# Sums of squares of q, k and the third layer's heads in two single passes

## The chip, the cores and the metric

The kernel runs on one core of a Trainium2 chip. A core has a matrix engine, TensorE (PE in the profile; its weight loads are PEld), and VectorE (DVE), ScalarE (ACT), GpSimd (POOL) and SyncE (SP), which issues the transfers. Each engine takes its instructions in its own order and waits on semaphores for the others. The metric is the time of one execution in device microseconds; less is better. Before the change it is 2625.27 us, the median of three runs (2624.19 to 2625.74).

## The reference

A stack of four layers on 1040 tokens (16 meta tokens and 1024 of the sequence) of width 1024, float32. Layers 0 and 3 are attention with a window of 128, layer 1 is an mLSTM, layer 2 an HGRN2 (a linear recurrence with gates). Each normalizes its input and adds its output to the stream h. What the change touches are normalizations of heads:

```python
def rmsnorm(x, g):
    xf = x.astype(jnp.float32)
    y = xf * lax.rsqrt(jnp.mean(xf * xf, axis=-1, keepdims=True) + EPS)
    return (y * g.astype(jnp.float32)).astype(x.dtype)
...
    # attention: 16 q heads and 4 k heads of 64
    q = rope(rmsnorm(q.reshape(bsz, lp, A_HEADS, A_HD), q_gain), pos)
    k = rope(rmsnorm(k.reshape(bsz, lp, A_KV, A_HD), k_gain), pos)
...
    # third layer: 8 heads of 128
    o = rmsnorm(o, o_gain.reshape(C_HEADS, C_DV)).reshape(bsz, lp, C_W)
```

## The kernel before

The stream is held transposed: 128 channels of a tile lie on the partitions, tokens along the free axis. Tokens are worked in three chunks of 400, 384 and 256 columns (for q in the last layer 384, 384, 256). A projection (`proj`) makes one tile of 128 output channels chunk by chunk; each chunk is 24 products of TensorE in four steps.

A product of float32 operands is taken at full precision. To go faster, most products are made from rounded parts: `split` has ACT round a tile to the type float32r (`h`) and DVE subtract that from the tile and round the rest (`l`), and three single passes (h by h, h by l, l by h) take the place of one full-precision product. Weights (`wh`, `wl`), the normalized input (`uh`, `ul`) and the operands of the output projections (`yh`, `yl`, three buffers each, `YS`) are made so. Split operands of the output projections are made by `ysplit` in `proj_out`.

A sum of squares over the channels of a head is a product of the squares with a matrix of ones, since the channels lie on the partitions. Before the change there are these:

- line 364, the norm of a layer's input, with `ones`, at full precision;
- line 516 (`stat_q`), q tiles: the squares of a block of 128 tokens are the stationary operand and two columns of the mask of heads the moving one, so the result has tokens on the partitions and two columns, one for each head of the tile; full precision;
- line 525 (`stat`), k tiles: the mask of heads (block diagonal, 128 by 128) by the squares of a chunk; full precision;
- line 983, the heads of the second layer: `ones` in float32r by two rounded parts of the squares, two single passes;
- line 1259 (`o_stat`), the heads of the third layer: `ones` by the squares, full precision.

TensorE's order is written out by hand: a list of steps with costs, into which other steps are put a given time after a chunk's end (`D_K` for k tiles, `D_Q` for q tiles, in the planner's ns, counted in the costs of the steps that stand between). For a k tile, the chunk's last product is followed by `evac` (ACT: line 492 scales, line 493 squares; four transfers turn halves for the rotation), after 2000 by `stat` (line 525, then Ln and Exp on ACT, lines 338 and 339), after 4000 by `rope` (DVE, lines 530 to 534, with a table `cs` that has one buffer), after 6000 by the turn (`k_split`: four casts and two copies on ACT, lines 444, 445 and 447, and two subtractions on DVE, line 446). For a q tile it is 2000 for the table, 3000 for `stat_q`, 4000 for `rope`, 6000 for the turn (`q_split`, lines 463 and 464). The factor that `stat_q` makes is read only in the scores of the softmax (line 629). The order on ACT, DVE, POOL and SP is made by a scheduler from the order of the steps and their priorities.

The first k tile and the first two q tiles of an attention layer are made in its head, together with the norm of the layer's input, chunk by chunk. A norm unit (`Norm.unit`, lines 386, 194, 195) makes `uh` and `ul` of one of eight tiles of a chunk. The second k tile is made later, between the softmax steps, its three chunks one right behind the other. In the third layer `o_evac` copies a head's output and squares it (lines 1251 and 1253), and `o_stat` follows at the next place for it.

Of the kernel before, what the change touches and what calls it, by code (L numbers as in the profile page):

```python
# [9 lines left out]
F32 = mybir.dt.float32  # L10
# [5 lines left out]
P = 128  # L16
# [29 lines left out]
D_V, V_AHEAD, K_AHEAD = 1500.0, 3000.0, 12000.0  # L46
PARTS = 4
FIRST = (0.2, 0.8, 0.85), (0.2, 0.75, 0.8)
D_K = 2000.0, 4000.0, 6000.0
D_Q = 2000.0, 3000.0, 4000.0, 6000.0  # L50


MM = 1.0 / 2.4
# [58 lines left out]
def hybrid_kernel(ctx: ExitStack, tc: tile.TileContext, ins, out, layers=(0, 1, 2, 3)):  # L112
# [41 lines left out]
    s.preload_act_table_set("natural_log_exp_and_others")  # L154

    ident = cpool.tile([P, P], F32, name="ident")
    ones = cpool.tile([P, P], F32, name="ones")
    v.memset(ones, 1.0)
    ngain = cpool.tile([P, 4, KT], F32, name="ngain")
    eps = cpool.tile([P, 1], F32, name="eps")  # L160
    v.memset(eps, EPS)
# [24 lines left out]
    def meta_tokens(mix):  # L186

        um[0] = z = mix.tile([P, KT, 48], F32R, name=nm("um"))
        g.memset(z.bitcast(F32), 0.0)
        for o, src in ((0, uh), (32, ul)):  # L190
            g.tensor_copy(z[:, :, o : o + NMETA], src[:, :, :NMETA].bitcast(F32))

    def split(src, h, l):
        s.copy(h, src)  # L194
# [98 lines left out]
    def proj_out(src0, src1, y, chunks=CHUNKS, fin=None, inrow=False):  # L293
        st = {}

        def pre0():
            st[0] = weights(src0, "o", inrow=inrow)

        def pre1():
            st[1] = weights(src1, "o", inrow=inrow)  # L300

        groups = []
        for n, (c0, cn) in enumerate(chunks):
            grp = []

            def ysplit(k, n=n, c0=c0, cn=cn):
                def fn():
                    yh, yl = (tpool.tile([P, 400], F32R, tag=z, name=nm(z), bufs=YS)[:, :cn] for z in ("yh", "yl"))
                    split(y(k)[:, c0 : c0 + cn], yh, yl)
                    st["y", n, k] = yh, yl  # L310

                return [0.0, hi(fn), None]

            def product(m, k, n=n, c0=c0, cn=cn):
                h, l = st[m // 4]
                mc = slice((m % 4) * P, (m % 4 + 1) * P)
                if k == 0:
                    st["p", n, m] = psj()
                acc = st["p", n, m]
                yh, yl = st["y", n, k]  # L320
                for i, (a, b) in enumerate(((h, yh), (h, yl), (l, yh))):
                    pe.matmul(acc[:, :cn], a[:, k, mc], b,  # L322
                              start=(k == 0 and i == 0), stop=(k == 1 and i == 2))
                if k == 1:
                    v.tensor_tensor(x[:, m, c0 : c0 + cn], x[:, m, c0 : c0 + cn], acc[:, :cn], op=ALU.add)  # L325
# [90 lines left out]
    def layer_a(i, j, first, last, fin):  # L416
# [3 lines left out]

        def enter():
            R["mix"] = mix = new_mix()
            R["masks"] = masks = mix.tile([P, 384], F32, name=nm("masks"))
            sp.dma_start(masks, ins["a_masks"])
            R["cons"] = cons = mix.tile([P, 18], F32, name=nm("cons"))
            sp.dma_start(cons, ins["a_cols"][j])
            v.tensor_scalar(cons[:, 0:1], cons[:, 0:1], -0.125, None, op0=ALU.mult)
            v.tensor_scalar(cons[:, 2:18], cons[:, 2:18], -1.0, None, op0=ALU.mult)
# [57 lines left out]
        def qk_proj(src, gcol, work, fsplit, ch, t=None):  # L486
# [11 lines left out]
            def finish(n, c0, cn):  # L498
                def factors():
                    b0, bn = CHUNKS[n]  # L500
                    if R.get("cs", (None,))[0] != n:
                        R["cs"] = n, R["mix"].tile([P, 2, 400], F32, tag="cs", name=nm("cs"), bufs=1)
                        sp.dma_start(R["cs"][1][:, :, :bn], ins["rope"][:, :, b0 : b0 + bn].rearrange("a p t -> p a t"))
                    late[n] += (R["cs"][1][:, :, c0 - b0 : c0 - b0 + cn],)

                def stat_q():

                    sq = late[n][1]
                    nb = len(CHUNK_BLOCKS[n])
                    R["rq", t, n] = rq = R["mix"].tile([P, 2 * nb], F32, tag=f"rq{n}", name=nm("rq"), bufs=4)  # L510
                    st = psa()
                    for k, b in enumerate(CHUNK_BLOCKS[n]):
                        if last and b == 0:
                            continue
                        q0 = blk(b)[0] - c0
                        pe.matmul(st[:, 2 * k : 2 * k + 2], sq[:, q0 : q0 + P], R["masks"][:, 0:P:64], start=True, stop=True)  # L516
                    z = slice(2 if last and n == 0 else 0, 2 * nb)
                    s.activation(rq[:, z], st[:, z], AF.Ln, bias=eps, scale=1.0 / 64)
                    s.activation(rq[:, z], rq[:, z], AF.Exp, scale=-0.5)

                def stat():
                    factors()
                    sq = late[n][1]
                    st = psa()
                    pe.matmul(st[:, :cn], R["masks"][:, 0:P], sq, start=True, stop=True)
                    rstd_from(st, sq, cn, 64)

                def rope():
                    dst, sq, rot, cos_sin = late[n]
                    v.tensor_tensor(dst, dst, cos_sin[:, 0, :cn], op=ALU.mult)  # L530
                    v.tensor_tensor(rot, rot, cos_sin[:, 1, :cn], op=ALU.mult)
                    v.tensor_tensor(dst, dst, rot, op=ALU.add)
                    if t is None:
                        v.tensor_tensor(dst, dst, sq, op=ALU.mult)

                turn = fsplit(lambda: late[n][0], n, c0, cn)
                if t is not None:
                    return [(D_Q[0], [0.0, factors, None]), (D_Q[1], [108 * len(CHUNK_BLOCKS[n]), stat_q, None]),
                            (D_Q[2], [0.0, rope, None]), (D_Q[3], turn)]
                return [(D_K[0], [4 * cn * MM, stat, None]), (D_K[1], [0.0, rope, None]), (D_K[2], turn)]  # L540

            return proj(src, evac, ch), [finish(n, *c) for n, c in enumerate(ch)]

# [51 lines left out]
        def mixers():  # L595


            def S_step(w):
# [27 lines left out]
                        g.tensor_copy(Sm[:nq, :, nk : nk + 1], cons[:nq, 2 + head : 4 + head].rearrange("p (u c) -> p u c", c=1))  # L626
                for u in range(2):
                    rq = R["rq", w["ts"][u], n][:nq, 2 * kq + hh : 2 * kq + hh + 1]
                    v.tensor_tensor_reduce(Sm[:nq, u, :nk], S[:nq, u, :nk], R["masks"][:nq, P + mo : P + mo + nk],  # L629
                                           rq, sinks[u], ALU.add, ALU.min, st[:nq, u : u + 1])  # L630
                for u in range(2):
                    s.activation(Sm[:nq, u, : nk + 1], Sm[:nq, u, : nk + 1], AF.Exp, scale=-1.0,  # L632
# [124 lines left out]
    def layer_b(i, j, fin):  # L757
# [3 lines left out]
        def enter():  # L761
# [10 lines left out]
            R["ones"] = mix.tile([P, P], F32R, name=nm("onesr"))  # L772
            s.copy(R["ones"], ones)
            R["G"] = mix.tile([P, NB, 16], F32, name=nm("G"))
            R["li"], R["lf"] = row(), row()

# [177 lines left out]
        def og_proj(h):  # L954
            st = {}

            def evac(c):
                def f(acc, n, c0, cn):
# [9 lines left out]
                    else:  # L968
                        q = R["sq", n]
                        s.activation(a[:, :cn], hr[:, cs], AF.Square)  # L970
                        v.tensor_tensor(q, q, a[:, :cn], op=ALU.add)
                        R["sqs", n] = qs = [tpool.tile([P, 400], F32R, tag=z, name=nm(z), bufs=YS)[:, :cn]
                                            for z in ("yh", "yl")]
                        split(q, *qs)
                return f

            def stat(n, c0, cn):
                def fn():
# [1 line left out]
                    q = R["sq", n]  # L980
                    sm = psa()
                    for i, z in enumerate(R["sqs", n]):
                        pe.matmul(sm[:, :cn], R["ones"], z, start=(i == 0), stop=(i == 1))
# [47 lines left out]
    def layer_c(i, j, fin):  # L1031
# [80 lines left out]
        def mixer(h):  # L1112
# [136 lines left out]
            def o_evac(n):  # L1249
                c0, cn = CHUNKS[n]  # L1250
                s.copy(R["o", h][:, c0 : c0 + cn], W["po"][:, :cn])
                W["sq", n] = sq = tmp()
                s.activation(sq[:, :cn], W["po"][:, :cn], AF.Square)

            def o_stat(n):
                c0, cn = CHUNKS[n]
                o, sq = R["o", h][:, c0 : c0 + cn], W["sq", n]
                st = psa()
                pe.matmul(st[:, :cn], ones, sq[:, :cn], start=True, stop=True)
# [7 lines left out]
            for r in range(5):  # L1267
# [10 lines left out]
                for b in range(len(REGIONS[r])):  # L1278
                    ts.append(S(427, tail2, r, b))
                    if REGIONS[r][b] in (5, 8):  # L1280
                        ts.append(S(666, o_stat, 0 if REGIONS[r][b] == 5 else 1))
                tails.append(ts)
            return main, tails, S(427, o_stat, 2)

        fg = {h: f_proj(h) for h in range(8)}
        qg = {h: q_proj(h) for h in range(8)}
# [96 lines left out]
    k = 0  # L1383
# [120 lines left out]
```

## Time and profile before

| | |
|---|---|
| median of three runs | 2625.27 us |
| profiled execution | 2624.74 us, its span 2623.0 us |
| PE busy | 2565.2 us, 98% |
| DVE busy | 1970.6 us, 75% |
| ACT busy | 1665.7 us, 64% |
| POOL busy | 249.8 us, 10% |
| mean granted clock of TensorE | 0.993 |

Shares of busy time are of the whole span; what a change in a stage is worth is read from that stage. A timeline row has the start in us from the span's start, the duration in us, the engine, the line, the operation, output and inputs, the shape and a count; in square brackets stands how long the engine was idle before it and what ended that. A row of a group ends with busy time, mean ns of one, and idle time ahead of it. A row of windows has the stretch, its length, the busy us of PE, PEld, DVE, ACT and POOL with counts, the granted clock, the transfers' share and GB/s. A full-precision product stands in the profile as two records of a load and a pass. Matmuls overlap, so their cost in a row of others is the distance between starts.

### The profile page before, as it was taken

The numbers are of one execution on the slowest core, as the hardware profiler recorded it, in microseconds if no ns is written. First come the engines' busy times: TensorE is split into PE (matmuls) and PEld (weight loads), VectorE is DVE, ScalarE is ACT, GpSimd is POOL, SyncE is SP. The second block draws the span as 40 slices with busy tenths as digits, with TensorE's granted clock in tenths as the row PEclk, the third lists the DMA queues.
The fourth block names the chain that finished last, engine by engine and source line by source line (L and its number), as shares of the span: only waits on it lengthen the run. The fifth ranks groups of instructions, "written<-read, shape, count | busy, mean of one in ns | idle before, by whom it ended". The sixth has DMA issues, their size and how long they took to land. (4 is left out here: it accounts for less than half of the span.)

```text
span 2623.0 us, 54248 instructions
## 1 busy us (share of the span) xinstructions
PE 2565.2 (98%) x20422; PEld 2484.6 (95%) x20422; DVE 1970.6 (75%) x5296; ACT 1665.7 (64%) x4374; POOL 249.8 (10%) x502
## 2 busy tenths in 40 slices
PE   7999999989999999999999999999999999999999
PEld 5999999989999999999999999999999999999999
DVE  6798798784747474747475688989787978887996
ACT  6776767565454545454545657878585857767772
POOL 2221221000000000000000000100000100321330
PEclk9999999999999999999999999999999999999999
DMA  4212111021111111111111101011110112212112
GB/s 129 68 50 84 55 44 48 22 66 49 42 56 41 57 41 56 42 53 45 53 45 49 49 26 50 26 42 34 34 42 30 38 51 86 59 50 84 55 39 79
DMA packets 82583, 135.92 MB, mean 52 GB/s; under 512 B 12033, under 2 KB 35713, under 8 KB 82321
## 3 DMA queue, kind: packets, MB, share of 16 engines
q1 hardware_dynamic: 82320, 132.45, 16.2%
q8 instruction: 161, 2.64, 0.4%
q14 instruction: 102, 0.83, 0.1%
HBM read 117.56 MB, written 4.26 MB: 46 GB/s over the span
## 5 line engine op out<-in xcount | busy, mean ns | idle before, releaser
L228 PE MATMUL pj<-uh,wh 128*128 128x256 f32 (+2 forms) x2688 | 916.4, 341 | 9.6 <-ACT uh L194 9.6
L228 PE MATMUL pj<-ul,wh 128*128 128x256 f32 (+2 forms) x2688 | 867.9, 323 | 2.2 <-DVE ul L195 1.7
L228 PE MATMUL pj<-uh,wl 128*128 128x256 f32 (+2 forms) x2688 | 864.6, 322 | 0.0
L228 PEld LDWEIGHTS pj<-uh,wh 128*128 128x128 f32 x2688 | 510.2, 190 | 26.8 <-ACT uh L194 13.2
L228 PEld LDWEIGHTS pj<-ul,wh 128*128 128x128 f32 x2688 | 510.5, 190 | 11.1 <-DVE ul L195 5.8
L228 PEld LDWEIGHTS pj<-uh,wl 128*128 128x128 f32 x2688 | 510.0, 190 | 0.0
L194 ACT CAST wh<-wr 128x512 fp32r<-128x512 f32 (+1 forms) x338 | 203.2, 613 | 110.9 <-PE pj L322 32.7
L195 DVE TENSOR_TENSOR wl<-wr,wh 128x512 fp32r<-128x512 f32 (+1 forms) x338 | 233.7, 701 | 51.6 <-ACT wh L194 49.3
L325 DVE TENSOR_TENSOR x<-x,pj 128x384 f32<-128x384 f32 (+2 forms) x480 | 234.7, 508 | 35.0 <-PE pj L322 33.7
L322 PE MATMUL pj<-yh,wh 128*128 128x384 f32 (+2 forms) x768 | 253.0, 329 | 8.0 <-DVE x L325 6.2
L322 PE MATMUL pj<-yh,wl 128*128 128x384 f32 (+2 forms) x768 | 245.2, 319 | 0.0
L322 PE MATMUL pj<-yl,wh 128*128 128x384 f32 (+2 forms) x768 | 245.2, 319 | 0.0
L277 PE MATMUL pj<-wh,uh 128*128 128x256 f32 (+1 forms) x768 | 231.9, 302 | 0.0
L277 PE MATMUL pj<-wl,uh 128*128 128x256 f32 (+1 forms) x768 | 216.5, 282 | 0.0
L277 PE MATMUL pj<-wh,ul 128*128 128x256 f32 (+1 forms) x768 | 216.2, 281 | 0.0
L635 POOL TENSOR_TENSOR Sm<-Sm,s 128x512 f32<-128x512 f32 (+2 forms) x136 | 142.1, 1045 | 449.4 <-DVE s L634 434.5
L632 ACT ACTIVATE Sm<-Sm,s 128x257 f32<-128x257 f32 (+2 forms) x272 | 130.9, 482 | 79.5 <-DVE s L629 75.3
L404 ACT ACTIVATE t<-t 128x384 f32<-128x384 f32 (+2 forms) x240 | 117.9, 491 | 87.8 <-DVE t L403 86.0
L403 DVE SCALAR_TENSOR_TENSOR t<-pj,t 128x384 f32<-128x384 f32 (+2 forms) x192 | 98.7, 514 | 80.0 <-ACT t L402 78.1
L322 PEld LDWEIGHTS pj<-yh,wh 128*128 128x128 f32 x768 | 144.2, 188 | 11.7 <-DVE x L325 7.4
L194 ACT CAST yh<-r 128x384 fp32r<-128x384 f32 (+2 forms) x120 | 57.1, 478 | 151.9 <-PE pj L322 139.8
L277 PEld LDWEIGHTS pj<-wh,uh 128*128 128x128 f32 x768 | 144.6, 188 | 2.1
(255 smaller groups left out, 5423.0 us busy)
## 6 DMA issues: line engine op xcount, KB each, us to landing
wr<-in_b_win SPq DMA_DIRECT2D x124, 256.0 KB, 2.8
wr<-in_a_win SPq DMA_DIRECT2D x80, 256.0 KB, 2.9
wr<-in_c_win SPq DMA_DIRECT2D x64, 256.0 KB, 2.8
wr<-in_a_wout SPq DMA_DIRECT2D x32, 256.0 KB, 2.8
wr<-in_b_wout SPq DMA_DIRECT2D x32, 256.0 KB, 2.8
t<-t SPq DMA_DIRECT2D x104, 48.0 KB, 1.9
cs<-in_rope SPq DMA_DIRECT2D x11, 400.0 KB, 3.4
cs<-in_rope SPq DMA_DIRECT2D x11, 384.0 KB, 3.6
```

Source lines behind the costliest of these rows:

```text
L194: s.copy(h, src)
L195: v.tensor_tensor(l, src, h.bitcast(F32), op=ALU.subtract)
L228: pe.matmul(acc[:, :cn], a[:, k, :], b[:, k, c0 : c0 + cn], start=(k == 0 and i == 0), stop=(k == KT - 1 and i == 2))
L277: pe.matmul(acc[:cn, :nc], a[:, k, c0 : c0 + cn], m[:, kk, :], start=(k == 0 and j == 0), stop=(k == KT - 1 and j == 2))
L322: pe.matmul(acc[:, :cn], a[:, k, mc], b, start=(k == 0 and i == 0), stop=(k == 1 and i == 2))
L325: v.tensor_tensor(x[:, m, c0 : c0 + cn], x[:, m, c0 : c0 + cn], acc[:, :cn], op=ALU.add)
L403: v.scalar_tensor_tensor(a[:, :cn], z, 0.0, a[:, :cn], op0=ALU.min, op1=ALU.subtract)
L404: s.activation(a[:, :cn], a[:, :cn], AF.Exp)
L632: s.activation(Sm[:nq, u, : nk + 1], Sm[:nq, u, : nk + 1], AF.Exp, scale=-1.0, bias=st[:nq, u : u + 1], accum_out=den[:nq, u : u + 1])
L635: g.tensor_tensor(Sm[:nq, :, :nk], Sm[:nq, :, :nk], den[:nq].rearrange("p (u c) -> p u c", c=1).to_broadcast([nq, 2, nk]), op=ALU.mult)
```

## The change

The squares of the q and k tiles and of the third layer's heads are split into two rounded parts (`parts_of`: a cast on ACT, a subtraction on DVE, into the yh/yl buffers that the output projections use), and the product with ones or with the mask of heads is taken in two single passes, as line 983 did it already. The part of the masks that is multiplied (`heads`) comes by a transfer of its own and is cast to float32r when a layer is entered; the constant of ones is held in float32r for the whole kernel, and read as float32 where it was. A k tile has its split at 500 and the statistic at 2500 (before: 2000); a q tile has the split at 2000 and the statistic at 5000 (before: 3000, ahead of the rotation at 4000). In the third layer the split follows the square in `o_evac`, and the planned cost of `o_stat` is halved.

```diff
-D_K = 2000.0, 4000.0, 6000.0
-D_Q = 2000.0, 3000.0, 4000.0, 6000.0
+D_K = 500.0, 2500.0, 4000.0, 6000.0
+D_Q = 2000.0, 5000.0, 4000.0, 6000.0
...
+    def parts_of(src, cn):
+        h, l = (tpool.tile([P, 400], F32R, tag=z, name=nm(z), bufs=YS)[:, :cn] for z in ("yh", "yl"))
+        split(src, h, l)
+        return h, l
...
-            R["masks"] = masks = mix.tile([P, 384], F32, name=nm("masks"))
-            sp.dma_start(masks, ins["a_masks"])
+            R["masks"] = masks = mix.tile([P, 256], F32, name=nm("masks"))
+            sp.dma_start(masks, ins["a_masks"][:, P:])
+            heads = tmp()[:, :P]
+            sp.dma_start(heads, ins["a_masks"][:, :P])
+            R["heads"] = mix.tile([P, P], F32R, name=nm("heads"))
+            s.copy(R["heads"], heads)
...
+                def squares():
+                    late[n, "sq"] = parts_of(late[n][1], cn)
...
-                        pe.matmul(st[:, 2 * k : 2 * k + 2], sq[:, q0 : q0 + P], R["masks"][:, 0:P:64], start=True, stop=True)
+                        for i, z in enumerate(late[n, "sq"]):
+                            pe.matmul(st[:, 2 * k : 2 * k + 2], z[:, q0 : q0 + P], R["heads"][:, 0:P:64],
+                                      start=(i == 0), stop=(i == 1))
...
-                    pe.matmul(st[:, :cn], R["masks"][:, 0:P], sq, start=True, stop=True)
+                    for i, z in enumerate(late[n, "sq"]):
+                        pe.matmul(st[:, :cn], R["heads"], z, start=(i == 0), stop=(i == 1))
...
-                    return [(D_Q[0], [0.0, factors, None]), (D_Q[1], [108 * len(CHUNK_BLOCKS[n]), stat_q, None]),
+                    return [(D_Q[0], [0.0, factors, None]), (D_Q[0], [0.0, squares, None]),
+                            (D_Q[1], [108 * len(CHUNK_BLOCKS[n]), stat_q, None]),
                             (D_Q[2], [0.0, rope, None]), (D_Q[3], turn)]
-                return [(D_K[0], [4 * cn * MM, stat, None]), (D_K[1], [0.0, rope, None]), (D_K[2], turn)]
+                return [(D_K[0], [0.0, squares, None]), (D_K[1], [2 * cn * MM, stat, None]),
+                        (D_K[2], [0.0, rope, None]), (D_K[3], turn)]
...
-                W["sq", n] = sq = tmp()
+                sq = tmp()
                 s.activation(sq[:, :cn], W["po"][:, :cn], AF.Square)
+                W["sq", n] = sq, parts_of(sq[:, :cn], cn)
...
-                pe.matmul(st[:, :cn], ones, sq[:, :cn], start=True, stop=True)
+                for i, z in enumerate(qs):
+                    pe.matmul(st[:, :cn], onesr, z, start=(i == 0), stop=(i == 1))
```

More of the change, by code (lines that the diff above doesn't have):

```diff
@@ L156, in hybrid_kernel @@
     ident = cpool.tile([P, P], F32, name="ident")
-    ones = cpool.tile([P, P], F32, name="ones")
+    onesr = cpool.tile([P, P], F32R, name="onesr")
+    ones = tmp()[:, :P]
     v.memset(ones, 1.0)
+    v.tensor_copy(onesr, ones)
+    ones = onesr.bitcast(F32)
     ngain = cpool.tile([P, 4, KT], F32, name="ngain")
@@ L307, in fn @@
                 def fn():
-                    yh, yl = (tpool.tile([P, 400], F32R, tag=z, name=nm(z), bufs=YS)[:, :cn] for z in ("yh", "yl"))
-                    split(y(k)[:, c0 : c0 + cn], yh, yl)
-                    st["y", n, k] = yh, yl
+                    st["y", n, k] = parts_of(y(k)[:, c0 : c0 + cn], cn)
                 return [0.0, hi(fn), None]
@@ L504, in factors @@
                     late[n] += (R["cs"][1][:, :, c0 - b0 : c0 - b0 + cn],)
+                def squares():
+                    late[n, "sq"] = parts_of(late[n][1], cn)
                 def stat_q():
-                    sq = late[n][1]
                     nb = len(CHUNK_BLOCKS[n])
@@ L628, in S_step @@
                     rq = R["rq", w["ts"][u], n][:nq, 2 * kq + hh : 2 * kq + hh + 1]
-                    v.tensor_tensor_reduce(Sm[:nq, u, :nk], S[:nq, u, :nk], R["masks"][:nq, P + mo : P + mo + nk],
+                    v.tensor_tensor_reduce(Sm[:nq, u, :nk], S[:nq, u, :nk], R["masks"][:nq, mo : mo + nk],
                                            rq, sinks[u], ALU.add, ALU.min, st[:nq, u : u + 1])
@@ L771, in enter @@
             R["hgain"] = cols[:, 80:96]
-            R["ones"] = mix.tile([P, P], F32R, name=nm("onesr"))
-            s.copy(R["ones"], ones)
             R["G"] = mix.tile([P, NB, 16], F32, name=nm("G"))
@@ L971, in f @@
                         v.tensor_tensor(q, q, a[:, :cn], op=ALU.add)
-                        R["sqs", n] = qs = [tpool.tile([P, 400], F32R, tag=z, name=nm(z), bufs=YS)[:, :cn]
-                                            for z in ("yh", "yl")]
-                        split(q, *qs)
+                        R["sqs", n] = parts_of(q, cn)
                 return f
@@ L982, in fn @@
                     for i, z in enumerate(R["sqs", n]):
-                        pe.matmul(sm[:, :cn], R["ones"], z, start=(i == 0), stop=(i == 1))
+                        pe.matmul(sm[:, :cn], onesr, z, start=(i == 0), stop=(i == 1))
                     rstd_from(sm, q, cn, 256)
@@ L1251, in o_evac @@
                 s.copy(R["o", h][:, c0 : c0 + cn], W["po"][:, :cn])
-                W["sq", n] = sq = tmp()
+                sq = tmp()
                 s.activation(sq[:, :cn], W["po"][:, :cn], AF.Square)
+                W["sq", n] = sq, parts_of(sq[:, :cn], cn)
             def o_stat(n):
                 c0, cn = CHUNKS[n]
-                o, sq = R["o", h][:, c0 : c0 + cn], W["sq", n]
+                o, (sq, qs) = R["o", h][:, c0 : c0 + cn], W["sq", n]
                 st = psa()
-                pe.matmul(st[:, :cn], ones, sq[:, :cn], start=True, stop=True)
+                for i, z in enumerate(qs):
+                    pe.matmul(st[:, :cn], onesr, z, start=(i == 0), stop=(i == 1))
                 rstd_from(st, sq, cn, 128)
@@ L1280, in mixer @@
                     if REGIONS[r][b] in (5, 8):
-                        ts.append(S(666, o_stat, 0 if REGIONS[r][b] == 5 else 1))
+                        ts.append(S(333, o_stat, 0 if REGIONS[r][b] == 5 else 1))
                 tails.append(ts)
-            return main, tails, S(427, o_stat, 2)
+            return main, tails, S(213, o_stat, 2)
         fg = {h: f_proj(h) for h in range(8)}
```

## The prediction

> **What bounds the kernel now.** I read the shares of busy time first, then the busy time by stage, then the groups by shape, the waits, and the timeline at each place where a sum of squares is taken.
>
> ```profile
> span 2623.0 us, 54248 instructions
> ...
> PE 2565.2 (98%) x20422; PEld 2484.6 (95%) x20422; DVE 1970.6 (75%) x5296; ACT 1665.7 (64%) x4374; POOL 249.8 (10%) x502
> ```
>
> TensorE (PE) is busy 98% of the span, and its order is written out by hand. What is taken from PE's work shortens the run; what makes PE wait lengthens it. The next view is busy time by stage: length, then PE, PEld, DVE, ACT, POOL, then the granted clock.
>
> ```profile
> 65.00:400.00 335.00, 329.21 (x2262) 318.17 (x2263) 282.49 (x769) 241.17 (x706) 83.52 (x132) 0.98 0.20 59
> 1560.00:2150.00 590.00, 581.52 (x7247) 557.68 (x7247) 505.95 (x1617) 439.67 (x1236) 47.88 (x133) 1.00 0.12 39
> 2180.00:2200.00 20.00, 20.00 (x118) 19.37 (x117) 19.80 (x46) 16.55 (x39) 0.00 (x0) 1.00 0.19 50
> ```
>
> In the first attention layer and in the third layer DVE is busy 84% and 86%. At the head of the last layer it has 0.2 us free in 20. Just there the change gives DVE and ACT more to do.
>
> **The change, part by part.** *Products removed.* The k tiles have 12 full-precision products (line 525, six in each attention layer), the third layer's heads 24 (line 1259); the profile records each as two. The third group, line 516, has two columns per product.
>
> ```profile
> L525 PE MATMUL pa<-r,masks x12: 378/484/498, 28.8 to 2207.0; 128*128 128x400 f32 x4, 128*128 128x384 f32 x4, 128*128 128x256 f32 x4
> L1259 PE MATMUL pa<-t,ones x48: 377/486/590, 1662.7 to 2129.4; 128*128 128x400 f32 x16, 128*128 128x384 f32 x16, 128*128 128x256 f32 x16
> L516 PE MATMUL pa<-masks,t x272: 165/251/354, 33.4 to 2478.6; 128*128 128x2 f32 x136
> ```
>
> A duration contains the overlap with its neighbours, so I take the pitch of starts, from the timeline:
>
> ```profile
> 1662.68 0.83 PE L1259 MATMUL pa<-t,ones 128*128 128x400 f32 x2
> 1663.04 0.59 PE L228 MATMUL pj<-uh,wh 128*128 128x256 f32 x1
> 1663.47 0.28 PE L228 MATMUL pj<-ul,wh 128*128 128x256 f32 x1
> 1663.59 0.28 PE L228 MATMUL pj<-uh,wl 128*128 128x256 f32 x1
> ...
> 1665.04 0.34 PE L228 MATMUL pj<-uh,wh 128*128 128x400 f32 x1
> 1665.22 0.35 PE L228 MATMUL pj<-ul,wh 128*128 128x400 f32 x1
> ```
>
> From the 400-column product to the second product after it pass 0.79 us. Two single passes of 400 columns (0.18 each) and one of 256 (0.12) take 0.48, so a pair saves 0.31 us. Scaled by columns, 384 saves 0.30 and 256 saves 0.20. There are 12 of each size: **-9.7 us**, all on PE's path. That two passes cost as much as one full-precision product can be left out: line 983 already makes such pairs in the second layer.
>
> *The q tiles' products* (136 of two columns) become 272 single passes, each with its weight load; before there were 272 loads and 272 passes already. I take 0, and 1 us either way, since a few ns on each of 272 are possible. Their place after the chunk moves from 3000 to 5000 in the planner's units. The factor they give is first read a segment later, so that move costs nothing; without that distance it would be up to 2 us at a chunk.
>
> *Splits added:* 84 (24 in the third layer, 48 for q, 12 for k), each a cast on ACT and a subtraction on DVE, as line 322's operands have them:
>
> ```profile
> L195 DVE TENSOR_TENSOR yl<-r,yh 128x384 fp32r<-128x384 f32 x48 | 28.3, 590 | 14.5 <-ACT yh L194 14.2
> L194 ACT CAST yh<-r 128x384 fp32r<-128x384 f32 x48 | 24.3, 510 | 58.2 <-PE pj L322 57.9
> ```
>
> That is at most 84 x 0.51 = 43 us for ACT and 84 x 0.59 = 50 for DVE, beside PE's 2565. The cover is PE's own work; where DVE is full it is thin. For the scattered places in the attention layers and the third layer I take +1 us, between 0 and 6. Both queues run in program order, so I read from the order of the changed program what stands ahead of each new split. Three places stand out, all on the k tiles, whose place for the statistic hardly moves (2000 to 2500).
>
> *Place one, head of the last layer.* Here the changed order puts the subtraction for k's first chunk behind all eight norm units of the next chunk, where line 530 stood before. The subtraction for the second chunk comes behind the eight units of the third and behind line 531 of the first q tile.
>
> ```profile
> 2186.46 0.83 PE L525 MATMUL pa<-r,masks 128*128 128x400 f32 x2
> 2191.14 0.57 DVE L530 TENSOR_TENSOR r<-r,cs 128x400 f32<-128x400 f32 x1
> 2196.59 0.81 PE L525 MATMUL pa<-r,masks 128*128 128x384 f32 x2
> 2202.79 0.55 DVE L531 TENSOR_TENSOR t<-t,cs 128x384 f32<-128x384 f32 x1
> ```
>
> So the first remainder is ready at 2191.1 + 0.6 = 2191.7, and PE stands there from 2186.5: 5.2 us. The second is ready at 2203.3 + 3 x 0.59 = 2205.1 (three subtractions are new in that stretch). PE would be there at 2196.6 + 5.2 - 0.3 = 2201.5: 3.6 more, 8.8 together. Behind the waiting product stand the norm's own product and the q tiles; all of PE waits. Part comes back, since DVE and ACT catch up meanwhile. Of the 3.3 us that PE waits at 2233 for v (quoted below) I give back 2.3, and the slow clock after it, 3.4. **+3.1 us**, between -3 (no new wait, the old one gone) and +8.8 (nothing comes back).
>
> *Place two, the second k tile of the first layer.* Its last chunk's cast now stands behind six casts of the first chunk's k.
>
> ```profile
> 252.90 0.81 PE L525 MATMUL pa<-t,masks 128*128 128x384 f32 x2
> 253.56 0.57 DVE L531 TENSOR_TENSOR t<-t,cs 128x400 f32<-128x400 f32 x1
> 255.66 0.38 ACT L493 ACTIVATE t<-pj 128x256 f32<-128x256 f32 x1
> 256.10 0.70 PE L525 MATMUL pa<-t,masks 128*128 128x256 f32 x2 [0.20 <-ACT t L493]
> 256.33 0.52 ACT L444 CAST r<-t 64x400 fp32r<-64x400 f32 x1
> 258.93 0.52 ACT L447 CAST r<-r 64x400 fp32r<-64x400 f32 x1
> ```
>
> The square ends at 256.04. To that come one more weight cast (0.6), the six casts (256.33 to 259.45, 3.1), an Exp (0.5), the cast (0.4) and the subtraction (0.4): 261.0. PE reaches its product six 400-column passes later than before and 0.3 sooner by the chunk ahead: 255.9 + 1.1 - 0.3 = 256.7. That is **+4.3 us**, in two pieces: the 384 chunk's subtraction stands behind line 531, ready at 254.1 + 0.6, where PE comes at 252.9 or a little later, so some 1.5 us there and 2.8 at the last chunk. Ends 0 and 6.
>
> *Place three, the same tile in the last layer.*
>
> ```profile
> 2393.25 0.39 ACT L493 ACTIVATE t<-pj 128x256 f32<-128x256 f32 x1 [0.16 <-DVE t L534]
> 2393.70 0.47 PE L525 MATMUL pa<-t,masks 128*128 128x256 f32 x1
> 2393.99 0.52 ACT L444 CAST r<-t 64x400 fp32r<-64x400 f32 x1
> 2397.08 0.56 DVE L532 TENSOR_TENSOR t<-t,t 128x384 f32<-128x384 f32 x1
> ```
>
> Six casts from 2393.99 (6 x 0.53), the cast and the subtraction end at 2398.0, the latter also behind line 532 (2397.6). PE comes at 2393.7 + 1.1 - 0.3 = 2394.5: **+3.5 us** in one piece, ends 0 and 5.
>
> *The clock.* Idle time on PE has a second price:
>
> ```profile
> 45.41 0.69 PE L228 MATMUL pj<-uh,wh 128*128 128x384 f32 x1 [2.90 <-ACT uh L194]
> 2236.57 0.55 PE L666 MATMUL po<-Ph,v 128*128 128x256 f32 x1 [3.31 <-DVE v L587]
> 2495.56 0.44 PE L322 MATMUL pj<-yh,wh 128*128 128x384 f32 x1 [2.16 <-DVE x L325]
> ...
> 43.00:54.00 11.00, 8.60 (x29) 8.29 (x30) 7.41 (x13) 9.12 (x22) 4.95 (x7) 0.54 0.20 53
> 2235.00:2242.00 7.00, 4.96 (x21) 4.70 (x22) 3.79 (x13) 3.16 (x10) 1.24 (x3) 0.52 0.22 59
> 2493.00:2504.00 11.00, 8.84 (x61) 8.53 (x60) 10.31 (x29) 5.25 (x18) 2.10 (x6) 1.00 0.01 1
> ```
>
> The clock is the third number from the end. After waits of 2.90 and 3.31 us it fell to about half, 7 us at 0.52 in the second case, which loses 7 x 0.48 = 3.4 us. After 2.16 us it did not. So place three pays 3.4, place two half of that (2.8 us lies between the cases), 1.7; at place one the slow stretch lies under the second wait. **+5.1 us**, ends 0 and 10. [...]
>
> *Buffers in the third layer.* The new splits use the three yh/yl buffers of the output projections. In two heads an output projection runs at the same time, and four of its splits get their buffer only 0.4 to 1.2 us (passes counted in the changed order, at the pitches above) ahead of PE's use. A cast and a subtraction take 1.1. The shortfalls add up to 1.5 us. ACT already waits 139.8 us for these buffers (second row; the first is a timeline row of the start):
>
> ```profile
> 31.60 0.91 PE L364 MATMUL pa<-r,ones 128*128 128x384 f32 x2 [1.98 <-POOL r L356]
> ...
> ACT yh L194 <- PE pj L322: 139.8, 55, 6.4
> ```
>
> I take **+2 us**, ends 0 and 4. The masks' second DMA, its cast and the constant's copy lie under PE's wait of 1.98 us for POOL at the start: 0, or 0.5 if that cover is gone.
>
> *Sum:* -9.7 + 0 + 1 + 3.1 + 4.3 + 3.5 + 5.1 + 2 = +9.3 us. The profiled execution took 2624.74 us (span 2623.0), 0.5 under the median of 2625.27; that gives **2634 us**.
>
> **The rivals.** *Faster.* The new remainders are in time at the three k places, because ACT and DVE reach them sooner than the old order's times say. Then only the last small terms stand against -9.7: -9.7 + 1 + 2 is 2618 us. It decides once the three places with their clock cost under 4.5 us instead of 16. For it: at place two the square itself is only 0.2 us late now. Against it: the order of the queues at the three places.
>
> *No change.* The waits come, but PE keeps its clock at places two and three: 2634 - 5.1 = 2629. [...] For it: place two's wait is in two pieces. Against it: the fall after 2.90 us.
>
> *Much slower.* Nothing comes back at the head of the last layer (+5.7), DVE, at 84 to 86%, delays more products (+5) and every place loses its clock (+5): 2650. For it: 0.2 us free in 20. Against it: PE has 20.0 busy there, so what is late now is little.
>
> **How the numbers follow.** Forecast (2630 to 2643 by its own ends) 0.44, faster 0.24, no change 0.20, much slower 0.12. A measurement of this kernel tells about 0.2%, 5.2 us, from no change: below 2620 is faster, above 2630.5 slower. So faster 0.24, same 0.20, slower 0.56. The range of 8 in 10 runs from 2616 to 2648.
>
> **What would show it.** Line 1259's successor as 48 passes of some 0.18 us pitch, with no wait ahead of them. PE idle for DVE's yl ahead of the k products near 2180 (5 us), 256 and 2390 (3 to 4 each). A granted clock near half behind these. No wait of 3 us for v in the last layer. DVE about 45 us busier. The prediction is wrong if PE's idle time ahead of the k products stays under 4 us in all, or if DVE falls behind in the third layer.

## The result

The changed kernel took 2655.57 us (median of 4 runs, 2654.78 to 2660.27) against 2625.51 for the kernel before, run beside it (2624.19 to 2628.28): a ratio of 1.0117, 95% interval 1.0099 to 1.0134. The forecast was slower, by 9 us; it is slower by 30. The profiled execution was the longest of the four, 2660.27 us. The ratios here and below leave out two single executions at a lower granted clock, of 2737 us at 0.881 (the kernel with the due time alone) and of 9508 us at 0.507 (the kernel before, beside it). Span and busy times of the changed kernel:

```profile
span 2658.5 us, 54397 instructions
...
PE 2567.6 (97%) x20422; PEld 2493.5 (94%) x20422; DVE 2015.2 (76%) x5381; ACT 1699.6 (64%) x4459; POOL 257.1 (10%) x502
```

DVE is 44.6 us busier, as foreseen, ACT 33.9. PE has as many records as before, 20422, and stands still longer. The waits of PE (what it waited for; us in total, times, longest), first of the kernel before, then of the changed one:

```profile
PE po L666 <- DVE v L587: 3.8, 2, 3.3
...
PE pt L647 <- POOL Sm L635: 2.5, 4, 1.2
...
PE pa L516 <- ACT t L493: 0.3, 1, 0.3
...
PE pa L525 <- ACT t L493: 0.2, 1, 0.2
```

```profile
PE pa L541 <- DVE yl L204: 8.6, 5, 4.9
PE pa L541 <- ACT yh L203: 8.3, 4, 3.4
PE pa L530 <- DVE yl L204: 7.2, 5, 2.8
PE pt L665 <- POOL Sm L653: 6.5, 7, 2.8
PE pj L329 <- ACT yh L203: 5.5, 3, 2.7
...
PE pj L329 <- DVE yl L204: 2.7, 4, 1.1
...
PE po L684 <- DVE v L605: 1.2, 1, 1.2
```

Line 541 is now the k statistic (525 before), 530 the q statistic (516), 329 the output projection (322), 665 the transposes of the softmax (647). Before, the two statistics waited 0.5 us in all and the projection never for its parts. Now the k statistic waits 16.9 us for the parts of its squares, the q statistic 7.2 and the projection 8.2.

Added over the whole trace, PE's idle times of more than 0.15 us came to 48.3 us before (46 of them) and 81.5 after (63). The time at half the granted clock went from 37.5 to 68.3 us, half of which is lost: 15.4 more. So 33.2 of idle time and 15.4 of clock, less the forecast's 9.7 for the products, make 38.9; the span grew by 35.5, and part of the slow stretches lies under waits.

The places, from the timeline of the changed kernel:

```profile
255.63 0.44 PE L541 MATMUL pa<-yl,heads 128*128 128x384 f32 x1 [0.86 <-DVE yl L204]
261.46 0.38 PE L541 MATMUL pa<-yh,heads 128*128 128x256 f32 x1 [2.12 <-ACT yh L203]
...
353.55 0.27 PE L530 MATMUL pa<-heads,yl 128*128 128x2 f32 x1 [2.50 <-DVE yl L204]
...
1860.04 0.45 PE L329 MATMUL pj<-yh,wh 128*128 128x400 f32 x1 [2.72 <-ACT yh L203]
1861.59 0.70 PE L329 MATMUL pj<-yl,wh 128*128 128x400 f32 x1 [1.11 <-DVE yl L204]
...
2205.63 0.70 PE L541 MATMUL pa<-yl,heads 128*128 128x400 f32 x1 [4.85 <-DVE yl L204]
2219.60 0.69 PE L541 MATMUL pa<-yl,heads 128*128 128x384 f32 x1 [2.10 <-DVE yl L204]
...
2254.25 1.11 PE L665 MATMUL pt<-ident,Sm 128*128 128x128 f32 x4 [2.79 <-POOL Sm L653]
...
2424.20 0.58 PE L541 MATMUL pa<-yh,heads 128*128 128x256 f32 x1 [3.37 <-ACT yh L203]
...
2517.38 0.37 PE L530 MATMUL pa<-heads,yl 128*128 128x2 f32 x1 [2.79 <-DVE yl L204]
```

The rows at 255 and 261 are place two, those at 2205 and 2219 place one, 2424 is place three. Those of lines 329 and 530 were in no step of the forecast with such sizes.

### The profile page after: what moved, and what is told of

The parts are those of the page before. It is cut to its first block, busy times and chain, and to the rows that moved or that the text cites. A ratio compares the mean times of both kernels' runs of the same rounds, so it can differ in the third digit from the quotient of the medians.

```text
span 2658.5 us, 54397 instructions
## 1 busy us (share of the span) xinstructions
PE 2567.6 (97%) x20422; PEld 2493.5 (94%) x20422; DVE 2015.2 (76%) x5381; ACT 1699.6 (64%) x4459; POOL 257.1 (10%) x502
## 4 chain that ended last, share of the span: by engine, by line
PE 76%; DVE 11%; ACT 8%; issue 2%; DMA 2%; POOL 1%; SPq 0%; DVEq 0%; ACTq 0%; POOLq 0%
PE pj L237 37%; PE pj L329 16%; PE pj L286 10%; PE po L684 2%; PE pt L665 1%; PE po L926 1%; ACT Sm L650 1%; PE pa L940 1%; PE po L928 1%; DVE Sm L647 1%; PE pj L282 1%; DVE wl L204 1%; PE pm L639 1%; PE pm L640 1%; ACT wh L203 1%
## 5 line engine op out<-in xcount | busy, mean ns | idle before, releaser
L329 PEld LDWEIGHTS pj<-yl,wh 128*128 128x128 f32 x768 | 146.9, 191 | 4.1 <-DVE yl L204 4.0
```

What stands on the lines that cost most here:

```text
L329: pe.matmul(acc[:, :cn], a[:, k, mc], b, start=(k == 0 and i == 0), stop=(k == 1 and i == 2))
```

## The experiments

Four questions: which of the three sums costs what; whether the price is PE's wait at the new passes, or the time of the splits on DVE and ACT, or the three yh/yl buffers; why the projection waits; and what is left of the change if the costs are avoided.

### One sum at a time

Two of the three statistics are put back to the full-precision product without a split; for k and q the old due times come back too. For the third layer alone, for instance:

```diff
-D_K = 500.0, 2500.0, 4000.0, 6000.0
-D_Q = 2000.0, 5000.0, 4000.0, 6000.0
+D_K = 2000.0, 4000.0, 6000.0
+D_Q = 2000.0, 3000.0, 4000.0, 6000.0
...
-                        for i, z in enumerate(late[n, "sq"]):
-                            pe.matmul(st[:, 2 * k : 2 * k + 2], z[:, q0 : q0 + P], R["heads"][:, 0:P:64],
-                                      start=(i == 0), stop=(i == 1))
+                        pe.matmul(st[:, 2 * k : 2 * k + 2], late[n][1][:, q0 : q0 + P], R["heads"].bitcast(F32)[:, 0:P:64], start=True, stop=True)
```

> Only the third layer's head statistics (24 products) go in two single passes; the k and q statistics keep their full-precision products and their old due times. Shared buffers (my theory after the result): the gain of the passes, 24 x about .27 = -6.5 us, is more than eaten by the output projection's parts, which share the three yh and three yl buffers: waits of the projection near 1857 and 2012 us of the changed kernel's profile with a half clock behind each, in all +8, so about 2633 us (2629 to 2637). Load alone (rival: the casts and subtractions only fill VectorE and ScalarE): no waits of the projection, 2619 to 2625. Passes no cheaper (rival): no gain near the ends of the heads, 2640 or more.

> Only the q statistics (two-column products) go in two passes; k and the third layer as before. Nothing can be gained on the matmul engine by these, so the time is pure price. Shared buffers and queue order: waits of the q statistic for yl as near 351 and 2509 to 2515 us in the changed kernel, about 2632 us (2627 to 2638). Load alone: 2625 to 2628.

> Only the k statistics (12 products) go in two passes with the split; q and the third layer as before. Queue order: the remainder's subtraction is late at the first layer's second tile (3 us), at the first two and the last tile of the last layer (4.9 + 2.1 and 3.4), with half clock behind, less 3.2 for the products: about 2640 us (2633 to 2649). Load alone: 2622 to 2627. The three of this call should add up to the whole change's +30.

Measured, against 2626.09 for the kernel before beside them: the third layer alone 2628.89 us (ratio 1.0011, 1.0001 to 1.0020), q alone 2645.44 (1.0069, 1.0054 to 1.0084), k alone 2637.18 (1.0041, 1.0026 to 1.0056). That is +2.8, +19.4 and +11.1, together +33.3 for the +30.0 of the whole. k came as expected. The third layer shows the expected waits (8.2 us at the projection) at 4 us less than expected, just under its range. q was a miss by 13 us: it can gain nothing, waits 8.9 us for its remainders, and costs more than twice that, nearly two thirds of the loss. (One more execution of q alone took 2645.45 us and waited 9.0 us there.)

One of these waits in q alone, in the timeline (cast, pass of the cast part, subtraction, pass of the remainder; line 204 is the subtraction of `split`, line 203 its cast):

```profile
2197.61 0.52 ACT L203 CAST yh<-t 128x384 fp32r<-128x384 f32 x1
...
2200.95 0.17 PE L530 MATMUL pa<-heads,yh 128*128 128x2 f32 x1
...
2204.09 0.55 DVE L204 TENSOR_TENSOR yl<-t,yh 128x384 fp32r<-128x384 f32 x1
...
2204.69 0.37 PE L530 MATMUL pa<-heads,yl 128*128 128x2 f32 x1 [3.57 <-DVE yl L204]
```

The cast part was there at 2198.1; the subtraction began 6.0 us later, though DVE was never idle in between: it stood behind the norm's units, the rotation of k and two weight splits. PE waited 3.57 us for a pass of two columns.

### The parts in other buffers

```diff
-                W["sq", n] = sq, parts_of(sq[:, :cn], cn)
+                W["sq", n] = sq, parts_of(sq[:, :cn], cn, ("t", "t"))
```

(and the same for the q and k squares; `parts_of` then takes both parts from the six temporaries `t`).

> The whole change, but the new parts are taken from the ring of six temporary tiles (t) in place of the three yh and three yl that the projections use. Shared buffers: the third layer's waits of the projection for its parts go, and with them up to 14 us; what stays is the late subtractions: about 2643 us (2636 to 2650). If the waits come from the place in the queues of ScalarE and VectorE and not from the buffers, 2653 or more; a new collision in the six temporaries could give that too, and would show as waits elsewhere.

It took 2707.34 us (1.0307, 1.0291 to 1.0322), 64 more than expected. The waits of PE there:

```profile
PE pa L530 <- ACT t L203: 31.8, 9, 5.6
PE pa L530 <- DVE t L204: 27.0, 11, 4.0
PE pa L541 <- ACT t L203: 9.6, 8, 3.1
```

The collision moved to the attention layers, where each chunk of q already takes temporaries: 59 us at the q statistic. In the third layer the projection no longer waits for its parts. As a whole this run can't tell the buffers from the queues, so the same was done to the third layer alone:

> Only the third layer's statistics in two passes, with their parts in the ring of temporaries, so that the projection keeps its three yh and yl for itself. Shared buffers (theory): the waits of 2.7, 1.1 and 2.6 us at the projection, and the half clock behind two of them, go: 2628.9 - 7 - up to 3 = 2620 us (2617 to 2625). If the third layer's waits come from the place in the queue: 2629 or more.

It took 2626.62 us (1.0003, 0.9994 to 1.0013), 6 us more than expected. The projection's waits for its parts are gone, so sharing yh and yl makes them. But the recurrence, whose `att` is summed through the same temporaries, now waits 6.4 us for it ahead of its products (1.0 in the kernel before); that the temporaries are the reason is likely, but was not tried by itself. A ring (buffers of one name that are handed out in turn) with room for one stage can lack it in another.

### The splits first in the queues

```diff
-                return [(D_K[0], [0.0, squares, None]), (D_K[1], [2 * cn * MM, stat, None]),
+                return [(D_K[0], [0.0, hi(squares), None]), (D_K[1], [2 * cn * MM, stat, None]),
```

(the same for q; `hi` is the priority that the projection's splits have).

> The whole change, with the casts and subtractions of the q and k squares issued with the same high priority that the projection's parts have, so that they stand ahead of the norm's and the weights' splits in the queues of ScalarE and VectorE. Place in the queue (theory): the matmul engine's waits for yl at the q and k statistics (about 9 us and 10 to 13 us in the profiles) go, with the half clock behind them; what stays is the third layer's +3 and the load: 2635 us (2629 to 2642). Buffers (rival: a split cannot start before an older yh or yl is free): no better than 2652.

It took 2639.18 us (1.0050, 1.0035 to 1.0065), 16 us less than the change as it stands. Line 530 does not wait for yl any more, and line 541 waits 4.8 us for it, at most 2.0 at a time. So rather more than half of the loss came from the place of the splits in the queues of ACT and DVE. Another 12.5 us stay, 4 more than I expected; the projection's waits (5.5 and 2.5 us) are among them, as expected.

### Splits that nothing reads

The q squares are split, but their statistic is the full-precision product of the square again, so that PE waits for no part (the two passes are left out). k and the third layer are as in the kernel before.

```diff
-                        for i, z in enumerate(late[n, "sq"]):
-                            pe.matmul(st[:, 2 * k : 2 * k + 2], z[:, q0 : q0 + P], R["heads"][:, 0:P:64],
-                                      start=(i == 0), stop=(i == 1))
+                        pe.matmul(st[:, 2 * k : 2 * k + 2], late[n][1][:, q0 : q0 + P], R["heads"].bitcast(F32)[:, 0:P:64], start=True, stop=True)
```

> The q squares are still split, at the new due times, but nothing reads the parts: the q statistic is the full-precision product again (the parts are left over, so the output is as before). Waiting at the passes (theory): the 8.9 us of waits for yl at the q statistic go, and with them most of q's +19: 2631 us (2627 to 2636). Load alone (rival): VectorE's and ScalarE's extra work makes the price, whoever reads the parts: 2640 us or more.

It took 2641.17 us (1.0056, 1.0041 to 1.0071): +14.5, where my theory by then said +5. Of q's 19.4 us only 4.3 go with the passes. Three things were left: the later due time, the splits' time on DVE and ACT, and their buffers. First the later due time by itself, in the kernel before, then the unread splits at the old due time:

```diff
-D_Q = 2000.0, 3000.0, 4000.0, 6000.0
+D_Q = 2000.0, 5000.0, 4000.0, 6000.0
```

> The kernel before with one number changed: the q statistic's due time, 3000 to 5000, as in the change. Nothing is split. If the price of the unused q splits (+14.5 us) is their load on VectorE and ScalarE (theory): within 3 us of before, 2623 to 2629. If it comes of the statistic's later place (rival): +10 us or more, 2636 or more.

> The unused q splits again, with the q statistic at its old due time of 3000. Load: as with 5000, 2636 to 2645. Due time: back to 2625 to 2630. The first and this one should add up to the +14.5 of both.

The due time alone gave 2628.73 (1.0004, 0.9995 to 1.0014), the unread splits at the old due time 2643.49 (1.0063, 1.0049 to 1.0077) against 2626.99. The second is 16.5 us over the kernel before, no less than with the new due time, so it is not the due time (the two do not add up to 14.5 either, as I had expected). Then the same splits with eight columns, so that count, places and buffers stay and the time goes:

```diff
-                    late[n, "sq"] = parts_of(late[n][1], cn)
+                    late[n, "sq"] = parts_of(late[n][1][:, :8], 8)
```

> The unused q splits once more, at the new due times, but of 8 columns only: the same number of casts, subtractions, buffers and places in the ring, with little of the engine time (the rest of each square is left unsplit; nothing reads the parts). Load: VectorE and ScalarE lose most of the 48 x about 0.5 us each that they had, and the time falls from 2641 to 2631 or less. Ring or queue places (rival): it stays at 2638 to 2643.

It took 2629.76 (1.0012, 1.0003 to 1.0022) against 2626.44, +3.3: some 11 of the 14.5 us go with the width. The busy times of the two, whole width first:

```profile
PE 2570.9 (97%) x20422; PEld 2488.5 (94%) x20422; DVE 1995.2 (76%) x5345; ACT 1686.7 (64%) x4423; POOL 251.3 (10%) x502
```

```profile
PE 2564.6 (98%) x20422; PEld 2483.1 (95%) x20422; DVE 1977.6 (75%) x5345; ACT 1675.1 (64%) x4423; POOL 248.8 (9%) x502
```

17.6 us of DVE and 11.6 of ACT, in engines that are 75% and 64% busy, cost some 11 us of the run, though no instruction reads what they make. Which of the two engines it is was not tried. The waits in the last layer (2180 to 2530) show how, again whole width first (line 538 is the k statistic here, 529 the q statistic):

```profile
PE pj L329 <- DVE x L332: 4.3, 3, 2.5
...
PE pa L538 <- ACT t L504: 2.8, 2, 2.6
PE pa L529 <- ACT t L504: 1.6, 1, 1.6
```

```profile
PE pj L329 <- DVE x L332: 2.5, 1, 2.5
PE pa L538 <- ACT t L504: 1.9, 1, 1.9
...
PE pa L529 <- ACT t L504: 0.4, 1, 0.4
```

Everything that ACT and DVE make in that stage comes a little later: the squares themselves (line 504) and the stream's sums that free the accumulators (332). Over the two whole traces PE's idle times of more than 0.15 us are 59.0 against 52.9 us, and half clock takes 23.9 against 17.1: together the 12.5 us between the two spans, within half a microsecond. So in these two profiles the waits make about half of the price, and the clock the other half.

All splits of the change, none of them read:

> The whole change's splits and due times, but every statistic is the full-precision product of the square again and nothing reads the parts (they are left over; the output is as before). Load: q's 14.5, and as the k splits lie in the same stages with 12 more splits against 48 parts, some 3 to 6 us more, the third layer's none; the products' gain is absent: 2644 us (2638 to 2652). Waiting at the passes: 2632 or less, since nothing waits for a part.

2644.04 us (1.0064, 1.0051 to 1.0078), the expected figure. Beyond q's 14.5, the k and third layer's splits cost some 3 without their passes. And the projection still waited for its parts, 5.0 us for yh (5.5 in the whole change) and 0.8 for yl (2.7), although the new parts were free as soon as they were made.

### Why the projection waits

The third layer alone, with two of the eight heads left at the full-precision product, first heads 4 and 6, in whose time PE's list holds an output projection:

```diff
-                W["sq", n] = sq, parts_of(sq[:, :cn], cn)
+                W["sq", n] = sq, parts_of(sq[:, :cn], cn) if h not in (4, 6) else None
```

> Third layer alone, in two passes for six heads of eight; heads 4 and 6, in whose time the output projection of the pair before runs, keep the full-precision product and take no yh or yl. Shared buffers: the projection's 8.2 us of waits for its parts go, 18 products still gain 0.28 each = 5.0 us: 2621 us (2618 to 2624), under the kernel before. If the splits' load or something else is the price in this layer: 2626 or more.

A miss: 2632.59 us (1.0019, 1.0010 to 1.0029), with all the projection's waits for its parts as they were (5.5 and 2.7 us). The code says why: the end of a head, with its statistic, is woven into the time of the next head, so that heads 3 and 5 stand beside the projections.

```diff
+                W["sq", n] = sq, parts_of(sq[:, :cn], cn) if h not in (3, 5) else None
```

> Third layer alone, with full-precision products for heads 3 and 5: each head's ends run in the time of the next head, so that these two, and not heads 4 and 6, have their statistics where the projection's parts are cast. Place in the ring (theory: a part of the projection can't be issued ahead of the statistics' parts that stand before it in the ring of three yh and three yl, even when these are free): the four waits at the projection (2.7, 1.1, 0.9, 2.6 us) go, its casts stand tens of us ahead as in the kernel before, and 18 products gain 0.28 each: 2621 us (2618 to 2625). Otherwise 2628 or more.

2619.70 us (0.9971, 0.9959 to 0.9982): less than both kernels, and PE waits for no part of the projection any more. With all heads it waited so:

```profile
PE pj L329 <- ACT yh L203: 5.5, 3, 2.7
...
PE pj L329 <- DVE yl L204: 2.7, 4, 1.1
```

The run without heads 4 and 6 left out the same number of splits and changed nothing at the projection, so it is not the amount of added work. The casts on ACT, first with all heads, then without heads 3 and 5:

```profile
1851.60 0.51 ACT L1262 ACTIVATE t<-po 128x384 f32<-128x384 f32 x1
...
1852.41 0.53 ACT L203 CAST yh<-t 128x384 fp32r<-128x384 f32 x1
1852.81 0.98 ACT L203 CAST yh<-r 128x400 fp32r<-128x400 f32 x2
```

```profile
1802.00 0.51 ACT L203 CAST yh<-r 128x400 fp32r<-128x400 f32 x1
1808.09 0.51 ACT L203 CAST yh<-r 128x400 fp32r<-128x400 f32 x1
```

The projection's rows `r` are ready long before. Without the statistic's parts ahead of them they are cast 45 to 51 us earlier. With them, they come right behind the cast of the square that precedes them in the ring of yh buffers, and that square is made only at 1851.6. So it is the place in the ring far more than how long a buffer is held: with parts that were free at once, 5.0 of the 5.5 us for the casts stayed (of the remainders' 2.7 only 0.8).

### What is left of the change

The k statistics alone with their splits first, and then these together with the third layer without heads 3 and 5; q stays at the full-precision product in both.

> Only the k statistics in two passes, with their splits at the high priority of the projection's parts. Place in the queue: of k alone's +11 the waits for yl (4.9 + 2.2 + 2.2 + 2.9 less what the whole change kept with it, 0.8 + 2.0 + 1.3) go, some 7 to 8 us and half clock behind them: 2627 us (2623 to 2631). Load alone: 2634 or more.

> The two before together, and no q: k statistics with their splits first, and the third layer's but for heads 3 and 5. The parts of the change that pay, if the theory holds: the sum of both, 2622 us (2618 to 2627).

k with its splits first took 2627.73 us (1.0003, 0.9994 to 1.0012): most of its +11.1 was the place in the queues. The k statistic's waits for its parts, first of k alone, then with the splits first:

```profile
PE pa L539 <- DVE yl L204: 8.1, 4, 4.8
...
PE pa L539 <- ACT yh L203: 5.1, 2, 2.9
```

```profile
PE pa L539 <- DVE yl L204: 2.5, 4, 1.6
...
PE pa L539 <- ACT yh L203: 0.4, 1, 0.4
```

The 2.9 us that are left are near the 3.2 that the 12 products give by the pitches, so k comes out about even; how much the splits' load takes besides was not tried by itself. Both together took 2620.11 (0.9969, 0.9957 to 0.9980), no more than the third layer alone. The version worth keeping is the third layer's two passes for six heads of eight, -6.7 us (the interval reaches from -4.7 to -10.8; 18 products at 0.28 make 5.0).

## Why the prediction was wrong

The sign was right, and at the three k places the mechanism too (parts late in the queues of ACT and DVE). The rest was not. Sorted by the three sums, the forecast is +12.8 for k (-3.2 for its products, the three places, the clock), -4.5 for the third layer (-6.5 + 2) and +1 for q and all other load; the runs of one sum at a time gave +11.1, +2.8 and +19.4. So the sum failed at q, which it held at nothing to gain and next to nothing to pay, and at the third layer's buffers. By the steps:

- *Products removed, -9.7:* right where it can be measured, in the third layer. From the first pass of a statistic to the second product after it pass 0.76 us in the mean of the 24 in the third layer before, 0.48 after: 24 x 0.28 = 6.7 us, where my pitches give 6.5. At k's 12 the waits hide it.
- *The q tiles' products, 0:* right for the passes (in the median 0.36, 0.59 and 0.81 us for a chunk of 2, 3 and 4 blocks before, 0.40, 0.59 and 0.81 after). But I looked for places where PE would wait only at the k tiles. The q statistic waits 7.2 us for its remainder in the changed kernel, 8.9 in q alone, of whose price 4.3 us went when the passes were left out.
- *Load on DVE and ACT, +1 (0 to 6):* the step that failed most. The 48 q splits cost some 11 us by their engine time alone. I wrote that the cover is thin where DVE is full, and still bounded its price by 6 us. All q and k splits lie in the first and the last layer, and DVE is busy 84% of the one (the stage 65 to 400 of the forecast) and 85% of the other (287.7 of the 340 us from 2180 to 2520).
- *Place one, +3.1:* the waits were sized well (4.85 and 2.10 us for 5.2 and 3.6), but what I gave back did not come. The wait for v fell from 3.3 us to 1.2; in its place came one of 2.79 for `Sm`, and the clock fell to 0.50 there all the same, for 6.8 us from 2253.4. The step's own upper end, +8.8, was nearer.
- *Place two, +4.3, and place three, +3.5:* 3.0 and 3.4 us measured, at the instructions that were named: right.
- *Clock, +5.1 (0 to 10):* 15.4 us of full clock lost in the profile. Half clock came at places one and three (3.4 us at 0.50 from each of 2205.6, 2219.3 and 2424.1), not at place two (1.00 from 253 to 264), and waits that were in no step brought slow stretches too (6.8 us at 0.50 from each of 1860.9, 2014.5 and 2516.3).
- *Buffers in the third layer, +2 (0 to 4):* the third layer alone gained 6.7 by its passes and still lost 2.8, so the price was 9.5. (In the profile of the third layer alone, from 1560 to 2150 us, PE idles 5.8 us longer than in the kernel before and half clock takes 3.4: 9.2 together.) I had counted how long a part must wait until its buffer is free. The runs show that the order of the ring takes away the 45 to 51 us by which the projection's parts could be cast ahead.
- *Masks' transfer, 0:* nothing in the runs speaks against it. It was not tried by itself.

The rival "much slower" (2650) named three of the causes: nothing given back, DVE delaying other products, and the clock lost everywhere. I gave it 0.12 because PE is 100% busy at the head of the last layer; that says what was covered before, not what the queues behind it could still take. It named neither q nor the ring; that its number came nearest is in part luck.

## What to carry to other kernels

DVE, 75% busy and off the critical path, was not free room: 17.6 us more of its time and 11.6 of ACT's, for splits that nothing reads, cost some 11 us. So ask for an engine's share in the stage where the work is added, and count also work that nobody waits for. When a new user takes buffers from a ring, look at what stood early in that ring and could be issued ahead of need; it now stands behind the newcomer's data. And a change in three places is worth taking apart: here one part pays once two heads are left out, one comes out even once its splits stand first, and one, which could gain nothing on the bounding engine, cost 19 us.

## What the runs showed of the hardware

The forecast priced the clock by the length of a wait. Two waits of nearly one length in the changed kernel speak against that: with 2.12 us ahead of line 541 at 261.46 the granted clock stayed at 1.00 (253 to 264), with 2.10 us ahead of 2219.60 it was 0.50 for 3.4 us from 2219.29 on. In the profiles of the two kernels, before and changed, all 34 changes of the granted clock lie at multiples of 3.413 us from each other (the largest remainder was 0.12% of that step), so PE's idle time was summed in each stretch between two such points that ran at full clock. After the 10 stretches with 2.0 us idle or more, the next was at half clock each time; after those with 1.5 to 2.0 in 4 of 11; with 0.5 to 1.5 in 2 of 57; with less, in none of 1436. A slow stretch was followed by another slow one in all 10 cases with 0.6 us idle or more, and in 2 of 15 with less than 0.3. These are counts of two profiles.

The cases agree with them. Of the 2.10 us ahead of 2219.60, 1.8 lie in one stretch; the 2.12 us ahead of 261.46 are cut into 0.7 and 1.4. Of the 2.60 us ahead of line 329 at 2014.83 in the changed kernel, 2.3 lie in one stretch, and the clock was halved for 6.8 us from the next on (the last row, its clock is third from the end). The 2.16 us ahead of 2495.56 in the kernel before are cut into 1.3 and 0.8, and the clock stayed at 1.00. So in these cases it mattered where a wait lay, beside its length.

```profile
2014.83 0.70 PE L329 MATMUL pj<-yh,wh 128*128 128x400 f32 x1 [2.60 <-ACT yh L203]
```

```profile
2014.50:2021.30 6.80, 6.47 (x19) 5.95 (x20) 4.72 (x11) 3.40 (x9) 0.92 (x4) 0.50 0.01 2
```
